# The bias strips of a dilated attention: 16 rows outermost in the load, copies outermost in the repeated table

## The chip, the core and the metric

The kernel runs on one core of a Trainium2 chip. A core has five engines that each work through their own list of instructions in order: PE (TensorE, matrix products), DVE (VectorE), ACT (ScalarE), POOL (GpSimd) and SP (SyncE, which here issues nearly all transfers). Transfers between DRAM and the on-chip memory run on 16 DMA engines beside them. The metric is the time of one execution of the whole program, in microseconds. The engines start and stop together, so a list that stands still early delays everything that is listed behind.

## The reference

One layer of a decoder for a prompt of 512 tokens and 8 sample tokens. One projection of x feeds two mixers, a gated linear attention (A) and a dilated window attention (B); the branches are gated, concatenated, projected and normalised. The part around the change is the position bias of mixer B:

```
def dilated_attention(q, k_all, v_all, q_idx, rel_bias):
    for window, dil in DILATED_GROUPS:                  # (128,1), (512,4), (2048,16)
        dist = jnp.arange(window // dil + 1, dtype=jnp.int32) * dil
        ...
        bias = rel_bias[t5_bucket(dist)].astype(F32).T
        logits = jnp.einsum('bqhd,bqjhd->bhqj', qf, kg) * scale + bias[None, :, None, :]
        ...
        p = jnp.exp(logits - m)
```

The bias of a query and a key depends on the head and on their distance alone. For 128 queries against a row of keys it is therefore a band: each query's row is the row before it, shifted by one.

## The kernel before

The projections run as matmuls over eight slices of 128 input features, each weight split in two parts (hi, lo) so that three matmuls give nearly full precision. A weight group of 128 columns is one load (raw_qb and the like, 512 KB, in packets of 512 bytes), then a cast on ScalarE (hi) and a subtraction on VectorE (lo), then 48 matmuls on TensorE for its two units (the first 264 tokens, then 256). The groups come in the order ka, qa, qb (four groups), kb (four), vb, gb, va, ga, then the output projection. Two raw buffers turn over, so a load waits until lo of the load two places ahead has been made. A matmul unit takes one of three banks of tag "d" and keeps it until its result has been copied out: for qb on ScalarE (qh), VectorE (ql) and, for the first unit, ScalarE again (q_s).

Between these, a planner (class Plan, lines 190 to 400 or so) puts the work of the other stages into the engines' lists. It runs while the program is built, with its own cost estimates, and each engine then keeps that order. In the stretch from 33 to 65 us that work is the gated attention's seven levels (gla_levels): VectorE forms differences d of the running sums b, ScalarE their exponentials, VectorE the scaled qs and ks, and TensorE the products ps_l.

The bias goes three steps. bias_table forms a row of 640 values for each of the 8 heads (tsb) and stores it to DRAM (tab, 8 rows of 2560 bytes). A second transfer copies tab to tabr, where each head's row stands 23 times (T_R = 23, T_P = 640). strips then loads, for each head and each half pi of the prompt, a strip of 128 partitions by w = 256 or 512 values from tabr. Partition p must read the head's row at a shift of -p. The load does this by two steps in DRAM: an inner step of T_P - 1 = 639, one copy further and one value back, and an outer step that does the same for whole groups of rows. The copies that are touched are numbered by the sum of both counters, 0 to 22 in either form, which is where the 23 copies come from. The operation that adds a strip to the scores and takes the maximum is V.tensor_tensor_reduce in softmax (pr<-ps_s,strip in the profile).

All these transfers are issued by SP, one after the other. Eight semaphores turn over among SP's transfers, so that an issue also waits until the transfer eight places earlier has landed. Nearly every operation shows line 359, since one helper records them all; the profile's rows are told apart by their tiles.

Of the kernel before, what the change touches and what calls it, by code (L numbers as in the profile page):

```python
# [30 lines left out]
HA, HB = 4, 8  # L31
# [19 lines left out]
T_P = 640  # L51
T_R = 23
# [7 lines left out]
    w=6, r=2,  # L60
# [129 lines left out]
class Plan:  # L190
# [18 lines left out]
    def mark(self, name):  # L209
        self.marks[name] += 1  # L210
# [4 lines left out]
    def free(self, *xs):  # L215
        for x in xs:
            name = x.tensor.name
            self.shares[name] = self.shares.get(name, 1) - 1
            if self.shares[name] == 0:
                last = {}  # L220
                for (_, eng), end in self.uses.pop(name, {}).items():
                    last[eng] = max(last.get(eng, 0.0), end)
                tag, (pool, t, _) = self.slot_of.pop(name)
                self.slots[tag].append((pool, t, last))
# [139 lines left out]
def trunk(ctx: ExitStack, tc: tile.TileContext, xT, xp, xs, state, ck, cv, w_in, wab, gnorm,  # L364
# [6 lines left out]
    T, V, S, G, D = (plan.engines[n] for n in ("PE", "DVE", "ACT", "POOL", "SP"))  # L371
# [10 lines left out]
    def bank(tag, name):  # L382
        return Need(tag, name, [P, 512])
# [18 lines left out]
    def copy(o, x):  # L402
        return V.tensor_copy(o, x), S.copy(o, x)
# [28 lines left out]
    tabr = dram.tile([HB, T_R, T_P], F32, name="tabr")  # L432
# [343 lines left out]
    def bias_table():  # L776
        yield At("const")
        tab = dram.tile([HB, T_P], F32, name="tab")
        raw = yield Need("g", "ct_raw", [66, T_D])
        yield D.dma_start(raw, c_t[:, :T_D])  # L780
        ct = yield Need("g", "ct", [66, T_D], F32R)
        yield V.tensor_copy(ct, raw)
        free(raw)
        tsb = yield Need("g", "tsb", [HB, T_P])
        yield V.memset(tsb[:, T_D:], NEG)
        yield At("rb")
        pt = yield bank("t", "ps_tab")
        yield T.matmul(pt[:HB, :T_D], rb[:, 0, :], ct, start=True, stop=True)
        yield copy(tsb[:, :T_D], pt[:HB, :T_D])
        free(pt)  # L790
        yield D.dma_start(tab, tsb)
        free(ct, tsb)
        yield D.dma_start(tabr, tab[:, None, :].to_broadcast([HB, T_R, T_P]))
        mark("tab")


# [292 lines left out]
    def strips():  # L1089
        yield At("tab")  # L1090
        yield At("qb", 1)
        for pi in range(2):
            w = 256 * (pi + 1)
            for h in range(HB):
                yield At(f"kb{h // 2}{pi}")
                strip = yield Need("st", f"strip{h}{pi}", [P, w])
                plan.share(strip, 2)
                B["strip", h, pi] = strip
                row = tabr[h]
                yield D.dma_start(strip, bass.AP(tensor=row.tensor, offset=row.offset + P - 1 + 512 - w,  # L1100
                                                 ap=[[T_P - 16, 8], [T_P - 1, 16], [1, w]]))
                mark(f"strip{h}{pi}")

    def scores(m, pi, qt):
# [476 lines left out]
    add(fills(), 9)  # L1581
    add(dense(), 100)
    add(bias_table(), 60)
    add(gla_levels(), 20)
    add(gla_diagonal(), 11)
    add(gla_state(), 24)
    add(gla_queries(), 25)
    add(strips(), 14)
    add(sample_queries(), 48)
    add(sample_softmax(), 2.5)  # L1590
# [116 lines left out]
```

## Time and profile before

| | |
|---|---|
| median of 3 runs | 290.79 us (290.52 to 290.88) |
| profiled execution, first to last instruction | 288.3 us, so 2.5 us under the median |
| granted TensorE clock, mean | 0.991 |
| DMA, bytes and packets | 51.18 MB in 58935 packets, mean 178 GB/s |
| strip loads | 8 of 128 KB and 8 of 256 KB, issued from 69.2 to 150.4 us |
| tabr, the repeated table | 460 KB in one transfer, issued at 24.1 us |
| tab, the table | 20 KB, issued at 21.4 us |

In the profile's rows "out<-in" names the tiles, "128x256 f32" partitions by elements, and a bracket at the end of a row of the timeline the idle time of the engine ahead of it and what ended it. In the rows of SP the two numbers ahead are the start of the issue and how long the issue took; the transfer itself runs later. A window's row on DMA counts the packets that started in the window. The row that begins with "DMA" and digits has the mean busy share of the 16 DMA engines in tenths in 40 equal slices, "GB/s" what they moved in each slice. In a row that begins with a window (280.00:281.00) stand its length, then busy time and number of instructions of PE, PEld, DVE, ACT and POOL, the granted clock, the DMA share and the GB/s.

### The profile page before, as it was taken

What the parts mean: (1) busy time and instruction counts of PE and PEld (TensorE: products, weight loads), DVE (VectorE), ACT (ScalarE), POOL (GpSimd) and SP (SyncE); (2) the same over time, 40 slices, a digit from 0 to 9 for tenths busy, and PEclk for the clock granted to TensorE, in tenths of its full rate; (3) what the DMA queues carried; (4) which work ended last, traced back from release to release, by engine and by line L of the source; (5) the groups of instructions that cost most, each with busy time, mean ns of one, the idle gap of its engine ahead of it and who ended that gap; (6) DMA issues with size and microseconds to landing.
All of it is one profiled execution on the core that took longest, in us unless ns stands there. A gap on an engine that the chain in (4) does not pass through costs nothing.

```text
span 288.3 us, 6893 instructions
## 1 busy us (share of the span) xinstructions
PE 275.0 (95%) x2636; PEld 259.7 (90%) x2636; DVE 228.9 (79%) x563; ACT 164.2 (57%) x462; POOL 57.2 (20%) x74
## 2 busy tenths in 40 slices
PE   8999999999999999999999998999999999999980
PEld 5899999998999998899999897999999999997880
DVE  3746897999889979979899997755888895339945
ACT  4747664455558767666969685436689774111000
POOL 4000001000592337303405545530000000000000
PEclk9999999999999999999999999999999999999996
DMA  7976522226957895659999998559745788641211
GB/s 204 275 188 183 155 75 75 75 77 138 356 173 216 254 271 193 182 170 225 273 205 184 192 220 238 145 142 244 224 82 156 229 280 242 109 152 51 99 75 73
DMA packets 58935, 51.18 MB, mean 178 GB/s; under 512 B 12554, under 2 KB 50196, under 8 KB 58902
## 3 DMA queue, kind: packets, MB, share of 16 engines
q1 hardware_dynamic: 58794, 50.66, 64.2%
q8 instruction: 21, 0.34, 0.5%
q14 instruction: 12, 0.10, 0.1%
q10 hardware_dynamic: 108, 0.07, 0.1%
HBM read 45.17 MB, written 6.03 MB: 178 GB/s over the span
## 4 chain that ended last, share of the span: by engine, by line
PE 66%; DVE 20%; ACT 5%; DMA 5%; issue 3%; SPq 0%; DVEq 0%
PE ps_qb L359 8%; PE ps_y L359 8%; PE ps_kb L359 7%; PE ps_ga L359 6%; PE ps_yf L359 4%; PE ps_qa L359 4%; PE ps_va L359 4%; PE ps_vb L359 4%; PE ps_ka L359 3%; PE ps_vb_f L359 3%; DMA raw_wo__3728<-in_w_out_dram 2%; DMA raw_ka<-in_w_in_dram 2%; PE ps_l L359 2%; PE ps_va_f L359 2%; DVE pr L359 2%
## 5 line engine op out<-in xcount | busy, mean ns | idle before, releaser
L359 POOL TENSOR_TENSOR vv<-vv,pb 128x256 f32<-128x256 f32 x32 | 27.0, 873 | 45.7 <-DMA pb<-psd_s 38.7
L359 POOL TENSOR_TENSOR past<-past,qbc 128x256 f32<-128x256 f32 x32 | 26.0, 849 | 42.0 <-DMA past<-in_ck_dram 36.5
L359 ACT ACTIVATE pr<-pr,ms 128x128 f32<-128x128 f32 (+3 forms) x49 | 26.1, 545 | 6.4 <-DVE ms L359 6.1
L359 PE MATMUL ps_pt<-cf,pr 128*128 128x128 f32 x80 | 13.8, 277 | 1.7 <-DVE ptl L359 0.9
L359 DVE CUSTOM_DVE_ANT_0 pr<-ps_s,strip 128x128 f32<-128x128 f32 (+3 forms) x32 | 14.3, 476 | 0.0
L359 PE MATMUL ps_ka<-xx,hi_ka 128*128 128x264 f32 (+1 forms) x64 | 13.6, 309 | 0.4 <-DVE xx L359 0.3
L359 ACT ACTIVATE sg<-sg 128x264 f32<-128x264 f32 (+1 forms) x32 | 13.4, 418 | 0.2
L359 PEld LDWEIGHTS ps_ka<-xx,hi_ka 128*128 128x128 f32 x64 | 11.1, 206 | 1.4 <-DVE xx L359 0.8
L359 ACT ACTIVATE d<-d 128x512 f32<-128x512 f32 x13 | 7.8, 636 | 6.7 <-DVE d L359 6.7
L359 PEld LDWEIGHTS ps_pt<-cf,pr 128*128 128x128 f32 x80 | 9.1, 140 | 2.7 <-DVE ptl L359 1.1
L359 DVE TENSOR_TENSOR ptl<-ps_pt,pth 128x384 fp32r<-128x384 f32 (+1 forms) x16 | 9.7, 615 | 1.6 <-ACT pth L359 1.6
L359 ACT ACTIVATE rstd<-mv 128x1 f32<-128x1 f32 x4 | 0.7, 199 | 17.5 <-DVE mv L359 17.5
L359 ACT COPY feat_y<-ps_yf 128x256 f32<-128x256 f32 x8 | 3.0, 371 | 13.2 <-PE ps_yf L359 13.2
L359 ACT CAST pth<-ps_pt 128x384 fp32r<-128x384 f32 (+1 forms) x16 | 8.4, 531 | 3.3 <-PE ps_pt L359 3.2
L359 POOL MEMSET att<- 64x512 f32 x2 | 1.0, 521 | 44.7 <-DVE ks L359 44.7
L359 DVE TENSOR_REDUCE o_pv<-vv 128x4 f32<-128x1024 f32 x8 | 9.7, 1210 | 0.0
L359 DVE TENSOR_REDUCE lt<-past 128x16 f32<-128x1024 f32 x8 | 9.6, 1199 | 0.0
L359 PE MATMUL ps_ka<-xx,lo_ka 128*128 128x264 f32 (+1 forms) x32 | 9.5, 295 | 0.0
L359 DVE TENSOR_TENSOR obT<-ps_pv,pvl 64x256 f32<-64x256 f32 x16 | 6.6, 414 | 3.3 <-ACT pvl L359 3.1
L359 DVE TENSOR_TENSOR xx<-x_raw,xx 128x520 fp32r<-128x520 f32 (+2 forms) x9 | 5.7, 640 | 3.8 <-ACT xx L359 3.8
L359 ACT COPY pvl<-ps_pv 64x256 f32<-64x256 f32 x16 | 5.5, 369 | 5.5 <-PE ps_pv L359 5.4
L359 DVE TENSOR_TENSOR d<-b 128x1024 f32<-128x1024 f32 x7 | 8.5, 1217 | 0.0
(535 smaller groups left out, 1093.3 us busy)
## 6 DMA issues: line engine op xcount, KB each, us to landing
past<-in_ck_dram SPq DMA_DIRECT2D x8, 512.0 KB
vv<-in_cv_dram SPq DMA_DIRECT2D x8, 512.0 KB
pb<-psd_s SPq DMA_DIRECT2D x16, 256.0 KB
qbc<-qsd SPq DMA_DIRECT2D x8, 256.0 KB
strip<-tabr SPq DMA_DIRECT2D x8, 256.0 KB
y<-in_xp_dram SPq DMA_DIRECT2D x4, 512.0 KB
x_raw<-in_xT_dram SPq DMA_DIRECT2D x7, 260.0 KB
out_dram<-y SPq DMA_DIRECT2D x3, 512.0 KB
```

The costliest lines, as they stand in the source:

```text
L359: getattr(eng.eng, op.fn)(*op.args, **op.kw)
```

## The change

Two lines change. The transfer that makes the repeated table has the 23 copies as its outermost dimension on both sides, in place of the 8 heads with the copies inside. The strip load has 16 rows outermost with an inner run of 8, in place of 8 with an inner run of 16; the outer step goes from 640 - 16 to 640 - 8 accordingly. Values, bytes and destination are the same in both.

```
@@ -790,7 +790,7 @@
         free(pt)
         yield D.dma_start(tab, tsb)
         free(ct, tsb)
-        yield D.dma_start(tabr, tab[:, None, :].to_broadcast([HB, T_R, T_P]))
+        yield D.dma_start(tabr.rearrange("h r t -> r h t"), tab[None, :, :].to_broadcast([T_R, HB, T_P]))
         mark("tab")
@@ -1098,7 +1098,7 @@
                 row = tabr[h]
                 yield D.dma_start(strip, bass.AP(tensor=row.tensor, offset=row.offset + P - 1 + 512 - w,
-                                                 ap=[[T_P - 16, 8], [T_P - 1, 16], [1, w]]))
+                                                 ap=[[T_P - 8, 16], [T_P - 1, 8], [1, w]]))
                 mark(f"strip{h}{pi}")
```

No instruction moves: the lists of PE, DVE, ACT and POOL are the same row for row. In SP's list one row reads differently, the one that writes tabr, among the loads of the qb weights (the sizes behind a name are those of the destination as the instruction holds them, outermost first):

```order
 L359 DMA tab<-tsb 8x640
 L359 DMA raw_qb__385<-in_w_in_dram 128x8x128
-L359 DMA tabr<-tab 184x1x640
+L359 DMA tabr<-tab 23x8x640
 L359 DMA raw_qb__434<-in_w_in_dram 128x8x128
 L359 DMA raw_qb__469<-in_w_in_dram 128x8x128
```

Before, the destination is 184 rows in one run, outermost; its source has 8 heads outermost and the copies as a step of zero inside. Now both sides have 23 outermost and 8 inside. The row stands at the same place in the list, between the loads for the second and the third qb group.

More of the change, by code (lines that the diff above doesn't have):

```diff
@@ L792, in bias_table @@
         free(ct, tsb)
-        yield D.dma_start(tabr, tab[:, None, :].to_broadcast([HB, T_R, T_P]))
+        yield D.dma_start(tabr.rearrange("h r t -> r h t"), tab[None, :, :].to_broadcast([T_R, HB, T_P]))
         mark("tab")
@@ L1100, in strips @@
                 yield D.dma_start(strip, bass.AP(tensor=row.tensor, offset=row.offset + P - 1 + 512 - w,
-                                                 ap=[[T_P - 16, 8], [T_P - 1, 16], [1, w]]))
+                                                 ap=[[T_P - 8, 16], [T_P - 1, 8], [1, w]]))
                 mark(f"strip{h}{pi}")
```

## The prediction

> **What bounds the kernel now.** I read the page first, for the busy shares and the chain of work that ended last.
>
> ```profile
> PE 275.0 (95%) x2636; PEld 259.7 (90%) x2636; DVE 228.9 (79%) x563; ACT 164.2 (57%) x462; POOL 57.2 (20%) x74
> DMA  7976522226957895659999998559745788641211
> PE 66%; DVE 20%; ACT 5%; DMA 5%; issue 3%; SPq 0%; DVEq 0%
> ```
>
> TensorE is busy for 275.0 of 288.3 us and holds 66% of the chain; DMA holds 5%. So a faster transfer helps only where somebody waits for it, and a TensorE stall is paid nearly in full. Both lines of the change are transfers, so the second view is the tiles: who uses a strip, and whether anyone waits.
>
> ```profile
> L359 DVE CUSTOM_DVE_ANT_0 pr<-ps_s,strip 128x128 f32<-128x128 f32 (+3 forms) x32 | 14.3, 476 | 0.0
> L359 SPq DMA_DIRECT2D strip<-tabr x16: 572/604/918, 69.2 to 150.4; - x16
> SPq L359 <- DMA strip<-tabr: 2.0, 2, 1.8
> ```
>
> The 32 operations that read a strip had VectorE idle 0.0 us before them: no strip was late. Only SP's queue waited for strips, 2.0 us in two waits, because an issue waits for the transfer eight places earlier. So **the strips' new pattern has almost nothing to win**, and the question is what the repeated table's write does to its neighbours. Third view: SP's timeline there.
>
> ```profile
> 23.65 0.37 SPq L359 DMA_DIRECT2D raw_qb__385<-in_w_in_dram  x1
> 24.11 0.78 SPq L359 DMA_DIRECT2D tabr<-tab  x1
> 27.28 0.37 SPq L359 DMA_DIRECT2D raw_qb__434<-in_w_in_dram  x1
> 30.56 0.37 SPq L359 DMA_DIRECT2D raw_qb__469<-in_w_in_dram  x1
> ```
>
> The table is written at 24 us and first read at 69.2 us, so its own lateness hurts nobody before 69. But weights for the third and fourth qb groups stand right behind it.
>
> **How many DMA engines a transfer gets.** Each engine that takes part closes its share with a 4-byte packet, and in a short window these are the packets under 512 B. Four windows, in order of time: the end of ct_raw (66 rows), the end of raw_qb__348 (128 rows) and tab (8 rows) together, the end of tabr, and raw_vb__1034 (128) with qsd (outermost 4).
>
> ```profile
> DMA packets 247, 0.18 MB, mean 313 GB/s; under 512 B 11, under 2 KB 217, under 8 KB 246
> DMA packets 231, 0.12 MB, mean 188 GB/s; under 512 B 24, under 2 KB 223, under 8 KB 231
> DMA packets 130, 0.08 MB, mean 265 GB/s; under 512 B 7, under 2 KB 122, under 8 KB 130
> DMA packets 564, 0.54 MB, mean 174 GB/s; under 512 B 20, under 2 KB 564, under 8 KB 564
> ```
>
> 66 rows gave 11 engines; 128 and 8 gave 16 + 8 = 24; 128 and 4 gave 16 + 4 = 20. For tabr, whose source has 8 outermost, 7 engines ended in that window and an eighth straggled. Each count is the largest number up to 16 that divides the outermost size. Now the table's write has 23 outermost on both sides, and 23 is prime: by this pattern **it runs on one engine**. The strips go from 8 outermost to 16, so from 8 engines to 16.
>
> No row here shows a prime size above 16. The Trainium skill, DMA: Bandwidth & Descriptors, section "Why a DMA increments its semaphore by 16 and not by 1", states this pattern as a rule for DMAs that SP issues, with 127 partitions on 1 engine; the trace's 66 rows on 11 agree. It also says that the GpSimd path may give uneven shares to all 16; by that the write would lose nothing, which is the second rival.
>
> **The change part by part.** The same 460 KB go out in the same 2560-byte packets; only the spread differs. Price per engine, from the speed by slices in the window 26.6 to 30.5 us, where tabr begins:
>
> ```profile
> GB/s 294 268 221 205 210 179 205 231 205 205 205 200 184 158 184 158 210 184 231 236 268 252 252 226 263 320 294 315 305 336 336 347 347 357 352 357 347 331 326 221
> GB/s 23 23 23 0 23 23 23 23 23 23 23 23 23 23 23 23 23 23 23 23 23 46 91 68 23 46 46 91 68 91 91 114 159 91 68 91 68 114 68 46
> ```
>
> Each slice is 0.1 us. The flow falls to 205 GB/s at about 26.7 us, when 8 engines have only tabr left: 205/8 = 25.6 GB/s each. On one engine 184 x 2560 B = 471 KB take 18.4 us, so tabr ends at 26.7 + 18.4 = 45.1 us instead of about 29.
>
> The second line (31.1 to 32.0 us) says what this does to the load behind it. A lone engine, late with tabr, moves raw_qb__434's 512-byte packets at 23 GB/s after the rest have finished: an engine serves its queue in order. So raw_qb__434's share on the one engine (32 KB, 1.4 us at 23 GB/s) ends at 46.5 us. From a weight load's last packet to its reader: raw_qb__385's late 4-byte packet is the only one under 512 B in the window 27.05 to 27.90 us, 0.3 to 1.2 us ahead of the cast that waited for it; I take 0.5.
>
> ```profile
> DMA packets 92, 0.17 MB, mean 204 GB/s; under 512 B 1, under 2 KB 30, under 8 KB 92
> 28.23 1.05 ACT L359 CAST hi_qb__445<-raw_qb__385 128x1024 fp32r<-128x1024 f32 x1 [0.40 <-DMA raw_qb__385<-in_w_in_dram]
> 33.50 1.04 ACT L359 CAST hi_qb__526<-raw_qb__434 128x1024 fp32r<-128x1024 f32 x1
> 34.81 1.22 DVE L359 TENSOR_TENSOR lo_qb__527<-raw_qb__434,hi_qb__526 128x1024 fp32r<-128x1024 f32 x1
> 37.08 0.42 DVE L359 SCALAR_TENSOR_TENSOR ql<-ps_qb,qh 128x256 fp32r<-128x256 f32 x1
> 43.54 0.68 DVE L359 TENSOR_TENSOR ks<-ka,d 128x512 f32<-128x512 f32 x1
> 42.57 0.40 PE L359 MATMUL ps_qb<-xx,hi_qb__445 128*128 128x256 f32 x2
> 45.02 2.07 PE L359 MATMUL ps_l<-qs,ks 64*64 64x32 f32 x128
> ```
>
> So hi_qb__526 starts at 47.0 instead of 33.50. The engines run in program order, and this is what queues behind the cast. **ScalarE** stands still until 48.0. **VectorE**'s lo_qb__527 then starts at 48.1 instead of 34.81: 13.3 us late, and with it ql, dg, qs, ks behind it; VectorE had almost no idle time from 34.81 to 45 us, so it catches nothing up. **TensorE** goes on with the second qb group, whose weights are there, until it needs a bank: there are three, and the unit that began at 42.57 takes the one that ql frees (37.08 + 13.3 = 50.4, plus the copy q_s on ScalarE). It resumes at about 51, has 2.45 us of matmuls to do, and then needs ks: 44.2 + 13.3 = 57.5 against 45.02. **TensorE is 12.4 us late** there.
>
> Nothing behind this point gives it back: VectorE, ScalarE and SP's later loads (each waits for a buffer that lo_qb frees) move by the same amount, and TensorE is full from 45 us on. raw_qb__469 needs 1.4 us more on that engine, 48 us in all, against its cast at 39.74 + 13: covered.
>
> **The clock.** TensorE pauses for some 8 us. What a pause and a restart do, from the end and the start of the span:
>
> ```profile
> 280.00:281.00 1.00, 0.30 (x3) 0.09 (x1) 0.62 (x2) 0.00 (x0) 0.00 (x0) 1.00 0.00 0
> 283.00:284.00 1.00, 0.00 (x0) 0.00 (x0) 0.96 (x3) 0.00 (x0) 0.00 (x0) 0.67 0.00 0
> 284.00:285.00 1.00, 0.00 (x0) 0.00 (x0) 0.96 (x2) 0.00 (x0) 0.00 (x0) 0.50 0.32 121
> 1.20 3.60 PE L359 MATMUL warm_ps<-warm 128*128 128x512 bf16 x8 [1.20 <-DVE warm L1576]
> 5.69 0.42 PE L359 MATMUL ps_ka<-xx,lo_ka 128*128 128x264 f32 x1
> 8.35 0.28 PE L359 MATMUL ps_ka<-xx,lo_ka 128*128 128x256 f32 x1
> ```
>
> Three us after the last matmul the granted clock fell to 0.50. At the start a matmul took 0.42 us at 5.69 us and 0.28 later, so the slow stretch lasted over 4.5 us from the first matmul. After the pause TensorE restarts slowly: 2.45 us of work become up to 4.9 us (51 to 56), still inside the wait that ends at 57.5. If it is still slow then, up to 4.9 us more at half speed lose up to 2.5 us. Ends: 0 and +2.5; I take +1.0, in between, since the slow work ahead of 57.5 may or may not be enough to bring the clock back.
>
> The Trainium skill, TensorE: Matmul & The Clock Gate, section "Part 1: The HAM clock gate", puts full clock after about 3.4 us of sustained work, and half clock after an idle window of that length. By it the clock may be back by 57.5 and the term be 0; the start's 0.42 us at 5.69 us speaks for a longer stretch here.
>
> **The strips.** Their share per engine halves, and nobody on the chain waited. Bounds: the 2.0 us that SP waited for strips on the one side (-1, as at most half of it comes back), nothing on the other. I take 0; what covers it is the gap between the issue at 69.2 and the first use at 76.8 us.
>
> **Sum.** 12.4 + 1.0 + 0 = 13.4 us. The profiled execution goes from 288.3 to 301.7 us; the median of the runs, 290.8, lies 2.5 us above the span, so 304.2 us; I say **304.0**.
>
> **Rivals.**
> 1. **The issue itself is held up.** If the one engine's queue has no room for 184 packets, SP cannot issue raw_qb__434 until it has drained. The issue at 27.28 to the end of that load (some 4 us, to 31.1) then follows 45.1: cast at 49.5, not 47.0, so 306.5 us. For it: nothing; tabr's issue took 0.78 us against 0.37 for a load. Against it: at 24 us raw_qb__385's 64 packets and tabr's 23 stood in one queue, and SP issued on; no row shows 184.
> 2. **The write is spread after all**, over 8 to 16 engines. Then nobody waits and the time is 290.8; with the strips' gain at its bound, 289.8. This is the end on the other side: faster by over 0.2% only if SP's 2.0 us of waiting return to the chain. Against it: 66 rows on 11 engines, which an uneven split would have put on 16.
> 3. **The change does nothing it says**: one engine, but the load behind isn't held (served in turn, or its last share not on that engine). Cover: raw_qb__434 was done by 32.0 us and its cast at 33.50 did not wait, so 290.8. Against it: the lone 23 GB/s row.
>
> **How the numbers follow.** One engine with the stall as summed: 0.80. Rival 1: 0.08. Rival 2: 0.05, of it 0.03 within 0.2% and 0.02 faster. Rival 3: 0.07, within 0.2%. About 0.2%, 0.6 us, is what a measurement here tells from no change. So slower 0.88, same 0.10, faster 0.02. The range: 304.0 less the clock's 1.0 and the strips' 1 is 302.0, less 0.5 for the start and speed of tabr; upward the clock's other 1.5 and rival 1's 2.5 without a second slow start: **301.5 to 307.0**.
>
> **What would show it.** The cast hi_qb__526 starts at about 47 us and waits for DMA raw_qb__434 some 13 us; VectorE and TensorE show matching holes (TensorE about 42.6 to 51 and up to 57.5); the window 30 to 44 us moves some 26 GB/s on one engine; ps_l at 57.4. Wrong if the cast does not wait, or if the hole at 45 is paid back by 130 us.

## The result and the profile after

The changed kernel takes 300.01 us (299.71 to 301.05, 5 runs) against 290.79 us before: a ratio of 1.0358, 95% interval 1.0321 to 1.0395. By the medians it is slower by 9.2 us; 13.2 were predicted, and the range began at 301.5. The ratio corresponds to 289.6 us for before, and so to a loss of 10.4 us: the five runs of before reach from 289.62 to 290.88 us, but for one of 294.56 in a slower state. The profiled execution took 300.65 us as a run, 1.75 us more than its span.

First the page of after, the rows whose counterparts of before stand in the prediction.

```profile
span 298.9 us, 6893 instructions
PE 276.2 (92%) x2636; PEld 261.2 (87%) x2636; DVE 226.1 (76%) x563; ACT 163.8 (55%) x462; POOL 54.4 (18%) x74
DMA  7973042322297679574999866866774688640311
PE 61%; DVE 12%; ACT 3%; DMA 2%; issue 1%; DVEq 0%; ACTq 0%
```

TensorE does the same 2636 matmuls in nearly the same busy time (275.0 before), but over a longer span: 92% instead of 95%. In the row of 40 slices (7.5 us each) DMA has 0 tenths in the fifth, from 30 to 37 us, where before it had 5. Next the timeline of SP, after.

```profile
23.90 0.37 SPq L359 DMA_DIRECT2D raw_qb__385<-in_w_in_dram  x1
24.36 0.73 SPq L359 DMA_DIRECT2D tabr<-tab  x1
27.53 8.97 SPq L359 DMA_DIRECT2D raw_qb__434<-in_w_in_dram  x1
36.59 6.23 SPq L359 DMA_DIRECT2D raw_qb__469<-in_w_in_dram  x1
49.94 0.37 SPq L359 DMA_DIRECT2D raw_kb__554<-in_w_in_dram  x1
```

And windows of 4 us of after.

```profile
30.00:34.00 4.00, 4.00 (x36) 4.00 (x36) 2.81 (x9) 2.56 (x8) 0.00 (x0) 1.00 0.07 26
46.00:50.00 4.00, 0.00 (x0) 0.00 (x0) 1.31 (x2) 1.33 (x2) 0.00 (x0) 0.75 0.05 15
50.00:54.00 4.00, 2.35 (x11) 2.35 (x12) 4.00 (x7) 2.43 (x5) 0.00 (x0) 0.50 0.48 131
54.00:58.00 4.00, 2.79 (x79) 2.55 (x78) 4.00 (x7) 1.60 (x4) 0.00 (x0) 0.89 0.10 15
58.00:62.00 4.00, 4.00 (x88) 3.96 (x89) 3.75 (x5) 2.37 (x4) 1.04 (x2) 1.00 0.42 120
```

From 30 to 34 us all transfers together move 26 GB/s with a DMA share of 0.07, about one engine of 16. The packet records show tabr's 184 packets of 2560 bytes one after the other from 27.20 to 45.73 us, 98.8 ns apart but for the first few. Then the engines' timelines of after, in the order ACT, DVE, PE.

```profile
47.61 1.04 ACT L359 CAST hi_qb__526<-raw_qb__434 128x1024 fp32r<-128x1024 f32 x1 [13.77 <-DMA raw_qb__434<-in_w_in_dram]
48.69 1.23 DVE L359 TENSOR_TENSOR lo_qb__527<-raw_qb__434,hi_qb__526 128x1024 fp32r<-128x1024 f32 x1 [13.59 <-ACT hi_qb__526 L359]
51.65 0.80 PE L359 MATMUL ps_qb<-xx,hi_qb__445 128*128 128x256 f32 x2 [8.67 <-ACT q_s L359]
52.24 0.41 PE L359 MATMUL ps_qb<-xx,lo_qb__446 128*128 128x256 f32 x1
54.80 0.31 PE L359 MATMUL ps_qb<-xx,lo_qb__446 128*128 128x256 f32 x1
57.97 1.14 PE L359 MATMUL ps_l<-qs,ks 64*64 64x32 f32 x64 [1.21 <-DVE ks L359]
```

The three stalls follow one from the other: ScalarE waits 13.77 us for the load right behind the table's write, VectorE 13.59 us for ScalarE, TensorE 8.67 us for a bank and then again for ks. Read with the windows: TensorE restarts at a granted clock of 0.50 (0.41 us per matmul), has 0.89 in the window to 58 us and 1.00 after it; in the trace the full clock begins at 54.85 us.

How late everything behind is, and whether it stays so, is read from three later casts, here on ScalarE's timeline of before:

```profile
61.72 1.05 ACT L359 CAST hi_kb__1027<-raw_kb__768 128x1024 fp32r<-128x1024 f32 x1 [0.44 <-PE ps_qb L359]
141.15 1.05 ACT L359 CAST hi_gb__2265<-raw_gb__2152 128x1024 fp32r<-128x1024 f32 x1
185.24 1.05 ACT L359 CAST hi_ga__2974<-raw_ga__2785 128x1024 fp32r<-128x1024 f32 x1
```

and on that of after:

```profile
73.93 1.04 ACT L359 CAST hi_kb__1027<-raw_kb__768 128x1024 fp32r<-128x1024 f32 x1 [0.43 <-PE ps_qb L359]
153.56 1.05 ACT L359 CAST hi_gb__2265<-raw_gb__2152 128x1024 fp32r<-128x1024 f32 x1
195.27 1.05 ACT L359 CAST hi_ga__2974<-raw_ga__2785 128x1024 fp32r<-128x1024 f32 x1
```

After is 12.2 us behind at 74 us, 12.4 at 154, but only 10.0 at 195, and 10.6 at the end (298.9 - 288.3). So the stall came as a whole, and some 2 us were given back between 154 and 195 us, a long way behind it. That is the part the prediction did not have. Two theories on it stood before the experiments: **A**, the wide strips pay it, since the pb and vv loads issued behind them no longer queue behind strips on eight engines, land sooner, and GpSimd's products collide less with VectorE; **B**, the strips do nothing and the shift gave the time back by accident.

### The profile page after: what moved, and what is told of

It is laid out like the page before. It is cut to its first block, busy times and chain, and to the rows that moved or that the text cites. A ratio compares the mean times of both kernels' runs of the same rounds, so it can differ in the third digit from the quotient of the medians.

```text
span 298.9 us, 6893 instructions
## 1 busy us (share of the span) xinstructions
PE 276.2 (92%) x2636; PEld 261.2 (87%) x2636; DVE 226.1 (76%) x563; ACT 163.8 (55%) x462; POOL 54.4 (18%) x74
## 4 chain that ended last, share of the span: by engine, by line
PE 61%; DVE 12%; ACT 3%; DMA 2%; issue 1%; DVEq 0%; ACTq 0%
PE ps_gb L359 8%; PE ps_y L359 8%; PE ps_ga L359 6%; PE ps_kb L359 4%; PE ps_yf L359 4%; PE ps_va_f L359 4%; PE ps_vb L359 4%; PE ps_va L359 4%; PE ps_pv L359 3%; PE ps_vb_f L359 3%; PE ps_pt L359 3%; PE ps_s L359 3%; DMA raw_wo__3728<-in_w_out_dram 2%; PE ps_oa L359 2%; PE ps_qb L359 2%; PE ps_l L359 1%
## 5 line engine op out<-in xcount | busy, mean ns | idle before, releaser
L359 POOL TENSOR_TENSOR vv<-vv,pb 128x256 f32<-128x256 f32 x32 | 25.2, 819 | 47.8 <-DMA pb<-psd_s 40.7
L359 POOL TENSOR_TENSOR past<-past,qbc 128x256 f32<-128x256 f32 x32 | 25.0, 814 | 40.7 <-DMA past<-in_ck_dram 37.9
L359 PE MATMUL ps_qb<-xx,hi_qb__445 128*128 128x264 f32 (+1 forms) x32 | 7.4, 329 | 8.7 <-ACT q_s L359 8.7
L359 DVE CUSTOM_DVE_ANT_0 pr<-ps_s,strip 128x128 f32<-128x128 f32 (+3 forms) x32 | 14.3, 475 | 0.0
L359 PEld LDWEIGHTS ps_qb<-xx,hi_qb__445 128*128 128x128 f32 x32 | 6.1, 232 | 8.9 <-ACT q_s L359 8.9
L359 DVE TENSOR_TENSOR lo_qb__527<-raw_qb__434,hi_qb__526 128x1024 fp32r<-128x1024 f32 x1 | 1.2, 1226 | 13.6 <-ACT hi_qb__526 L359 13.6
```

The source lines that it names most:

```text
L359: getattr(eng.eng, op.fn)(*op.args, **op.kw)
```

## The experiments

Each ratio is to the kernel before, run on the same chip; before had a median of 289.6 us beside the first four, 290.38 beside the next four, 290.2 beside the last three.

**Each half alone.** The strip line of the change alone:

```
-                                                 ap=[[T_P - 16, 8], [T_P - 1, 16], [1, w]]))
+                                                 ap=[[T_P - 8, 16], [T_P - 1, 8], [1, w]]))
```

> Only the strip load has its new pattern (16 rows outermost); the repeated table is written as before, heads outermost. Theory A (the wide strips give back some 2 us late in the kernel, because pb and vv no longer queue behind strips on eight engines, so that GpSimd multiplies vv earlier and collides less with VectorE): 288.3 to 289.3 us against 290.8, with no hole at 34 to 51 us, and the second group of vv products 2 us earlier than before against its neighbours. Theory B (the strips do nothing; the 2.4 us given back between 150 and 178 us are an accident of the shift): 290.5 to 291.1.

Measured: 288.51 us (12 runs), ratio 0.9978 (0.9956 to 1.0001). Not separable from no change by itself, on the side of A.

The table line alone:

```
-        yield D.dma_start(tabr, tab[:, None, :].to_broadcast([HB, T_R, T_P]))
+        yield D.dma_start(tabr.rearrange("h r t -> r h t"), tab[None, :, :].to_broadcast([T_R, HB, T_P]))
```

> Only the repeated table is written with its copies outermost; the strips load as before, 8 rows outermost. Both theories: the table's 184 packets go out on one engine, the cast hi_qb__526 waits about 13.8 us for raw_qb__434, and the operations at 50 to 70 us are 12.2 us late. Theory A: nothing or little is given back at 150 to 178 us, so 302 to 303 us. Theory B: the same is given back as with both lines, so about 300.0.

Measured: 302.17 us (6 runs), ratio 1.0425 (1.0394 to 1.0457), 12.6 us above before. The whole stall is in this line: the cast hi_qb__526 begins at 47.19 us after 13.87 us of waiting. And this kernel does not give back. On its ScalarE timeline:

```profile
73.51 1.05 ACT L359 CAST hi_kb__1027<-raw_kb__768 128x1024 fp32r<-128x1024 f32 x1 [0.41 <-PE ps_qb L359]
155.10 1.05 ACT L359 CAST hi_gb__2265<-raw_gb__2152 128x1024 fp32r<-128x1024 f32 x1
199.52 1.05 ACT L359 CAST hi_ga__2974<-raw_ga__2785 128x1024 fp32r<-128x1024 f32 x1
```

Against before these are 11.8, 13.95 and 14.3 us late, and the span is 301.8, so 13.5 at the end. With the same shift and narrow strips nothing comes back: this speaks against B. It is one trace, the slowest of its six runs; the runs say the same more faintly, as the intervals of this ratio and of the change's (up to 1.0395) no more than touch.

**The number of copies.** If the stall comes from 23 being prime, a few more copies must remove it, though more bytes are written. Both lines of the change, and

```
-T_R = 23
+T_R = 24
```

> Both lines of the change, but 24 copies instead of 23 (the last one is written and never read); everything else, and the order on all engines, is that of the changed kernel. If the stall comes from 23 having no divisor up to 16 but one, 24 outermost gives 12 engines: the table's 192 packets take 16 x 0.1 = 1.6 us per engine, the cast does not wait, and the time is that of the strips alone (theory A 288.3 to 289.3, theory B 290.5 to 291.1). Rival: copies outermost, or a step of zero outermost, are slow in themselves, or a 23 x 8 shape spreads evenly and something else stalls: about 300.

Measured: 288.41 us (12 runs), ratio 0.9957 (0.9936 to 0.9979). On ScalarE's timeline and SP's:

```profile
33.09 1.04 ACT L359 CAST hi_qb__526<-raw_qb__434 128x1024 fp32r<-128x1024 f32 x1
...
26.87 0.38 SPq L359 DMA_DIRECT2D raw_qb__434<-in_w_in_dram  x1
```

The cast waits for nothing, and the issue isn't held up. One more copy takes away the whole stall.

The other direction, 29 copies (also prime; the planner's cost of this transfer is held at that of 23, so that no instruction moves):

```
-T_R = 23
+T_R = 29
```

> Both lines of the change with 29 copies, prime again (six copies are written and never read); the planner's cost of that transfer is held at that of 23, so that the order on all engines stays. 232 packets on one engine at 0.0988 us are 22.9 us instead of 18.2: raw_qb__434's cast starts 4.7 us later, near 52.4 us, and the whole takes 304.7 us. Rival (the stall has a fixed length, or is not the transfer's own length): 300.0.

Measured: 305.02 us (4 runs), ratio 1.0548 (1.052 to 1.0577). ScalarE's timeline and SP's:

```profile
52.37 1.04 ACT L359 CAST hi_qb__526<-raw_qb__434 128x1024 fp32r<-128x1024 f32 x1 [18.26 <-DMA raw_qb__434<-in_w_in_dram]
...
27.79 13.46 SPq L359 DMA_DIRECT2D raw_qb__434<-in_w_in_dram  x1
```

Six more copies are 48 more packets of 98.8 ns, 4.7 us; the cast comes 4.8 us later and the kernel is 5.0 us slower than after (on another chip), 4.5 us in the profiled spans. Within what the runs can tell, the price per packet of the one engine is paid in full.

And 32 copies, which 16 divides, with the same held cost:

```
-T_R = 23
+T_R = 32
```

> Both edits as in the change, but the table has 32 copies instead of 23 (655 KB written instead of 471 KB), a number that 16 divides. If the stall came from 23 being prime, this write spreads over 16 engines, takes about 655 KB / (16 x 25.6 GB/s) = 1.6 us, nothing waits for the load behind it, the cast hi_qb__526 begins near 33 us and the time is that of the strips alone and of 24 copies: 287.5 to 289.5 us. If the number of copies as such, or the pattern with copies outermost, costs the time, it is 301 us or more. Against 24 copies (12 engines) it should differ by less than 0.7 us either way, since neither write is waited for.

Measured: 288.21 us (12 runs), ratio 0.9939 (0.9905 to 0.9973). As expected, no different from 24 within what can be told. The two versions beat both kernels, before by 0.4 and 0.6%.

**The place of the write.** The same write on one engine, but four loads later in SP's list, behind raw_kb__634:

```
 L359 DMA raw_qb__385<-in_w_in_dram 128x8x128
-L359 DMA tabr<-tab 23x8x640
 L359 DMA raw_qb__434<-in_w_in_dram 128x8x128
 L359 DMA raw_qb__469<-in_w_in_dram 128x8x128
 L359 DMA raw_kb__554<-in_w_in_dram 128x8x128
 L359 DMA raw_kb__634<-in_w_in_dram 128x8x128
+L359 DMA tabr<-tab 23x8x640
 L359 DMA raw_kb__768<-in_w_in_dram 128x8x128
```

> Both edits as in the change, 23 copies on one engine, but this write stands four loads later in SP's list: behind raw_kb__634 instead of ahead of raw_qb__434. The work and the number of bytes are those of the change. Theory 'place' (the stall is what the load right behind the write loses against its due time): raw_qb__434's cast is back near 33 us; the one engine is now busy from about 46 to 64.5 us, raw_kb__768, issued at 51.1 and due at 61.7, lands there at about 64.8, so a stall of 0 to 4 us near 62 us is left, and with 1.7 us given back by the strips the time is 288.5 to 292. SP's issue of raw_kb__768 is held up for some 4 to 9 us. Theory 'cost of the write itself' (one-engine writing slows the memory or the chip, wherever it stands): 299 to 302.

Measured: 294.28 us (6 runs), ratio 1.0148 (1.01 to 1.0196). The size missed, above the 288.5 to 292; the direction is that of "place", as some three fifths of the loss (1.5% instead of 3.6%) are gone with the same write. ScalarE's timeline:

```profile
66.37 1.05 ACT L359 CAST hi_kb__1027<-raw_kb__768 128x1024 fp32r<-128x1024 f32 x1 [5.37 <-DMA raw_kb__768<-in_w_in_dram]
```

The write landed at 64.75 us, close to the 64.5 of the estimate, but the load's own share on that engine follows and came at 66.27: the expectation had left out most of that 1.5 us. SP's issue of raw_kb__768 took 3.94 us, just under the 4 to 9 expected. The cast is 4.65 us behind before (61.72), VectorE then 4.4 us, and 6.0 us by 86 us. In this trace 1 us of that increase lies at one wait: TensorE had paused, its granted clock was 0.50 from 69.6 to 76.4 us, matmuls at 75 us took 0.41 us instead of 0.28, and VectorE waited 0.81 us for a product (ps_kt) that stood behind them; from there on it was 5.4 us late.

**Another queue.** The same write at the same time, issued by ScalarE into its own queue:

```
-        getattr(eng.eng, op.fn)(*op.args, **op.kw)
+        getattr(getattr(op, "queue", eng.eng), op.fn)(*op.args, **op.kw)
...
+        op = D.dma_start(tabr.rearrange("h r t -> r h t"), tab[None, :, :].to_broadcast([T_R, HB, T_P]))
+        op.queue = nc.scalar
+        yield op
```

> Both edits as in the change, 23 copies on one engine and at the same time, but the write is issued by ScalarE into its own queue instead of SP's. Theory 'in order in one queue': the packets of raw_qb__434 now stand in another queue of the same engine, so they no longer wait for all 184; taking turns packet by packet (64 of them beside 64 of the write at 98.8 ns) they land at about 36 to 38 us instead of 47.6, the cast hi_qb__526 is 3 to 5 us late, raw_qb__469 some 2 to 6 us, and the time is 291 to 296. SP's issue is not held up (0.4 us for raw_qb__434 instead of 9). Theory 'the engine itself serves the earlier write first': the cast stays at about 47 us and the time at 299 to 301.

Measured: 296.29 us (4 runs), ratio 1.0211 (1.0161 to 1.026). SP's timeline and ScalarE's:

```profile
27.18 0.37 SPq L359 DMA_DIRECT2D raw_qb__434<-in_w_in_dram  x1
29.95 0.37 SPq L359 DMA_DIRECT2D raw_qb__469<-in_w_in_dram  x1
...
39.53 1.05 ACT L359 CAST hi_qb__526<-raw_qb__434 128x1024 fp32r<-128x1024 f32 x1 [6.03 <-DMA raw_qb__434<-in_w_in_dram]
47.52 1.04 ACT L359 CAST hi_qb__610<-raw_qb__469 128x1024 fp32r<-128x1024 f32 x1 [2.97 <-DMA raw_qb__469<-in_w_in_dram]
```

The load's last share lands at 39.51 us instead of 47.59, while the write ends later, at 49.76 instead of 46.07: the engine now takes turns between two queues. The stall falls from 13.8 to 6.0 us, with 3.0 more at the next load, 9.0 in all. So about a third of the waiting (and two fifths of the loss in time, 2.1% instead of 3.6%) was order within one queue; the rest is sharing one engine. The last share came 1.5 us later than the upper end expected, and the time lies 0.3 us above its range.

**The strips the other way.** The table as before, the strips on 4 engines (35 copies, which this pattern needs, with the planner's cost held):

```
-                                                 ap=[[T_P - 16, 8], [T_P - 1, 16], [1, w]]))
+                                                 ap=[[T_P - 32, 4], [T_P - 1, 32], [1, w]]))
```

> The table as before the change (heads outermost, 8 engines, 35 copies that this pattern needs), the strips with 4 rows outermost instead of 8 or 16, so on 4 engines. Theory A (narrow strips hold the pb and vv loads behind them, wide ones release them): the other way round from the strips alone, slower than before: the second halves of pb land later still, GpSimd's wait for pb grows above 17 us, and the time is 291.5 to 297. Theory B (the strips do nothing for the time and the 1.7 us came by chance of the shift): within 0.5 us of before, 289 to 290.5.

Measured: 296.45 us (6 runs), ratio 1.0228 (1.0182 to 1.0275). The time is A's; the place is not. The waits from 104 to 116 us:

```profile
ACT pvl L359 <- DMA out_dram<-feat: 4.5, 1, 4.5
DVE l L359 <- DMA sel<-in_c_f_dram: 4.3, 1, 4.3
```

Neither wait is among the rows of before for this stretch. That output and sel are issued shortly behind two strips, and are late now: the issue that follows these strips, a qbc load, took 3.03 us instead of 0.68, and sel was issued at 106.98 us instead of 103.52. VectorE was 0.8 us behind before at 100 us, so the larger table is not the cause, and 5.1 us behind it after the wait for sel. In the run with the table line alone, where the strips are narrow too, VectorE waits 1.0 us for sel at the same place. A had said that GpSimd's wait for pb would grow; it did not (37.1 us in all, 38.7 before). So the pattern of a strip is paid by whatever is queued behind it, and not by its own readers, who waited 0.0 us here too.

**Which strips.** The last five loads stand ahead of pb and vv; the first eleven do not. Wide patterns for one part alone (k is 8 in the wide form; the condition is turned round for the early ones):

```
+                plan.strips = getattr(plan, "strips", 0) + 1
+                k = 8 if plan.strips > 11 else 16
...
-                                                 ap=[[T_P - 16, 8], [T_P - 1, 16], [1, w]]))
+                                                 ap=[[T_P - k, 128 // k], [T_P - 1, k], [1, w]]))
```

> The table as before the change; of the 16 strip loads only the last five (issued from about 120 us on, right ahead of pb and vv loads) have 16 rows outermost, the first eleven keep 8. Theory A (wide late strips let the pb and vv loads behind them land sooner, GpSimd's products then lie less on VectorE's operations at 150 to 180 us): the whole gain of the strips alone is here, 288.0 to 289.3 us where before is 290; VectorE gets through the instructions that took it from 150 to 180 us before in 27.3 to 28.5 us instead of 30.0, with some 2 us less busy time. Theory B (the strips do nothing, the gain comes by chance): no different from before, 289.5 to 290.5, 30 us for that stretch.

> The other half: only the first eleven strip loads (issued up to 101 us) have 16 rows outermost, the last five keep 8. Theory A: no gain, since no load that is waited for stands behind those: 289.5 to 290.5 us, and about 30 us for the instructions that took VectorE from 150 to 180 us before. Theory C (a wide strip is worth the same everywhere, some 0.1 us each): about 289. Theory B: as before.

> The strips alone once more, all 16 of them with 16 rows outermost, on the same chip as the two halves, so that the three compare: 288.0 to 289.3 us by theory A, the ratio below 1 and equal to that of the late five; 27.7 us for VectorE's stretch. If the first time was chance: ratio 1.0.

Measured, 12 runs each: the late five 288.94 us, ratio 0.9952 (0.9929 to 0.9975); the early eleven 289.99 us, ratio 1.0003 (0.9976 to 1.003); all sixteen 288.82 us, ratio 0.9971 (0.9946 to 0.9995). So the late five alone have the gain, as A says, and the early eleven show none, though the intervals of the two only just miss each other; B would have 1.0 in all three.

What did not come out is A's place for it in VectorE's list. A expected VectorE's instructions of 150 to 180 us to take 27.3 to 28.5 us with late or all strips wide, and 30 with the early ones. They took 30.0 us before, 27.2 with the late ones, 27.4 with all, but 27.8 with the early ones too, whose median gained nothing. That one profiled execution was the fastest of its twelve (288.70 us), as those of the other two were of theirs, so a single trace is not enough to place a gain of 1.5 us among executions that scatter by as much.

What A says of the pb loads did come out. The third set of GpSimd's vv products waits for a pb load that is issued at 142 us in before, behind two of the late strips; its row before, and with the late five wide:

```profile
152.76 3.69 POOL L359 TENSOR_TENSOR vv<-vv,pb 128x256 f32<-128x256 f32 x4 [9.93 <-DMA pb<-psd_s]
...
150.20 3.00 POOL L359 TENSOR_TENSOR vv<-vv,pb 128x256 f32<-128x256 f32 x4 [8.38 <-DMA pb<-psd_s]
```

From the issue of that load to these products it takes 10.8 us before and 8.5 with the late five wide. In all nine traces with wide late strips it is 8.3 to 10.0 us, in all four with narrower ones (before, table_only, early_strips, strips4) 10.5 to 11.3. That VectorE is done sooner because of it is likely but not shown: its stretch took 27.1 to 28.0 us in the nine and 27.8 to 30.0 in the four.

## Why the prediction was wrong in size

The mechanism that the prediction named is there, and by its own signs: the cast waited 13.77 us, 26 GB/s flowed meanwhile, and the hole was not paid back by 130 us. The time lies 4.2 us under the 304.2 of the sum, 1.5 us below the range, because three later terms were mis-sized.

**One engine for the write: right.** 26 GB/s at a DMA share of 0.07, tabr landed at 46.07 us (45.1 predicted), and 24, 29 and 32 copies behave as divisors say: 12 engines, one, 16 (so many shares of the write land in their traces).

**The load behind it: right.** The cast came at 47.61 us (47.0), lo_qb__527 at 48.69 (48.1), TensorE was back at 51.65 (51) and past its wait for ks at 57.97 (57.5). The offset that stayed on ScalarE and VectorE is 12.2 us where **12.4** was predicted for TensorE. That it is so close is in part luck, as two errors cancel: VectorE was 13.7 us late at ks and not 13.3, but of the 128 ps_l products at 45.02 us it is the second 64, at 45.98, that need the new ks, so that TensorE had 1 us more in hand.

**The clock, +1.0: wrong, it is about 0.** TensorE came back at half clock as predicted, but the slow work lay wholly within the wait that ended at 57.97 us: matmuls took 0.41 us from 51.65 on and 0.31 by 54.80, and TensorE was idle for the last 1.21 us of the wait. The row taken as evidence for a longer slow stretch, the first matmuls of the program at 5.69 us, did not carry over. Here the Trainium skill, TensorE: Matmul & The Clock Gate, section "Part 1: The HAM clock gate", with its 3.4 us of sustained work, is close to the trace (some 3.2 us from 51.65 to 54.85). Where the slow matmuls stand ahead of something that is waited for, the term is real: with the write four loads later it was about 1 us, as read from its trace.

**The strips, 0 with a bound of -1: wrong, this is the step of the mechanism that failed.** In the profiles the give-back is 1.65 us (from 12.2 to 10.6). Not all of it need be the strips, as before's own execution was slow in that stretch: the execution with only the early strips wide got through it 2.2 us faster too. In the runs, by the ratios, the strips alone are worth 0.6 and 0.8 us (0.9978 and 0.9971), the late five 1.4 (0.9952), and table_only lies 2.2 us above after, though on another chip. The prediction priced the strips by who waits for a strip, 2.0 us of SP. It should have asked, as it did for the table, what stands behind them in the queues. The sentence that nothing behind the stall gives it back also fell: it looked at the engines' lists and not at what the other edit does there. That pb lands sooner behind wide strips is shown in the traces, and that narrow ones hold up loads that are waited for by strips4; how the sooner pb shortens VectorE's work stays open.

**From span to median, +2.5: too much, and nothing in the range stood for it.** Every run took 1.7 to 1.95 us more than its span. The rest of the 2.5, some 0.7 us, was the distance of that one execution of before from its median, which has no reason to hold after the change. After's own median lay 0.64 us below its profiled run, 1.1 above its span. The ratio says the same, as it corresponds to 289.6 us for before and not to the 290.8 that the sum started from. So of the 4.2 us between 304.2 and 300.0, 0.2 are the stall, 1.0 the clock, 1.65 the strips, and 1.4 this conversion. The range had the clock at 0 and the strips at -1 at its lower end; what put the time below it is the strips' part beyond that, up to 0.65 us, and the 1.4 of the conversion, the larger of the two (against them stands 0.5 us that the range kept for the write's start and speed, of which the stall used 0.2).

**The rivals.** Rival 1 had its premise and not its result. SP's issue of raw_qb__434 was held up for 8.97 us, which the prediction had given little chance; but it went through at 36.50 us, nine microseconds ahead of the end of the write, and the load's other 15 shares had landed by 39.67, so the last share still followed tabr directly (47.59 us). Rival 2 fell with the 26 GB/s; rival 3 with the wait of 13.77 us.

## What to carry to other kernels

When a transfer's outermost size changes, count on how many engines it will run, and price it by what stands behind it in those queues and when that is due; its own readers may wait 0.0 us and the kernel still lose 12. A size with a good divisor is worth more bytes: one more copy (24 for 23) took the whole loss away. The same question goes for an edit that looks free in the waits, since wide strips let loads behind them land sooner; and a single profiled execution's distance to the median does not carry over to the changed kernel.

## What the runs showed of the hardware that was not expected

An issue can be held by the engine's backlog. Behind 184 packets on one engine raw_qb__434's issue took 8.97 us, behind 232 of them 13.46 us, and 0.37 where the write stood in ScalarE's queue. In both held cases it went through when 93 packets of the write were left, counted in the packet records: 91 of 184 had started at 36.50 us, and 139 of 232 at 41.25. raw_qb__469 went through at 42.82 us, when 29 of the write and the 64 of raw_qb__434 were left, 93 again. With the write four loads later it was 97 both times (at 54.78 us 97 of the write, at 61.10 us 33 and 64). SP issued nothing else in that time, so other loads, even for idle engines, wait with it. In the changed kernel that cost nothing, as the load on the slow engine was later still; with the strips on four engines the late issue of sel did cost.

Two queues on one engine take turns rather than first come, first served: raw_qb__434's 64 packets of 512 bytes were through 8.1 us sooner when the 184 stood in another queue, and these ended 3.7 us later. The packet records show the turns one by one: from 33.3 us on a packet of 512 bytes and one of 2560 alternate, a pair every 122 ns.
